# A diffusion layer on one core: the pairs' weight operands in a queue of their own, x's second half modulated on ScalarE, output weights requested one by one

## Chip, core and metric

The kernel runs on one core of one Trainium2 chip. The core has five engines that run their own instruction streams and meet at semaphores: TensorE (PE, matmuls and transposes; its weight loads are shown as PEld), VectorE (DVE), ScalarE (ACT), GpSimd (POOL) and SyncE (SP), which here issues nearly all transfers (DMA). The metric is the device time of one execution in microseconds (us); of several executions the median is taken. A profile of one further execution shows when each instruction ran, for how long, and what ended its engine's idle time before it.

## The reference

One layer over a context of 256 tokens and 2048 latent tokens of width 1024, all in fp32. Cut to what matters:

```python
ada = silu(c) @ w_ada + b_ada                       # six blocks: sh1 sc1 g1 sh2 sc2 g2
h = rmsnorm(x, norm_mix) * (1 + sc1) + sh1          # x: (1, 2048, 1024)
p = h @ w_in                                        # 1024 -> 3584: f, b, v, q, g (512 each), u, v of the gMLP
# head group A: 4 heads of HGRN2, gated linear recurrence, forward and backward, from the context's end states
o_hg = rmsnorm(o_f + flip(o_b), hg_norm) * silu(g)
# head group B: 4 heads of gMLP on chunks of 128 positions
o_mlp = gelu(u) * (W_s @ layernorm(gelu(v)) + b_s)
x = x + g1 * (concat(o_hg, o_mlp) @ w_out)
h2 = rmsnorm(x, norm_ffn) * (1 + sc2) + sh2
a, g = split(h2 @ w_up)                             # 1024 -> 2 x 2816
x = x + g2 * ((a * gelu(conv3x3(g) + conv_b)) @ w_down)
return rmsnorm(x, norm_final)
```

## The kernel before

Matmul operands are split into a high and a low part, each of a short fp32 format (`split`, lines 131 to 134: a cast on ScalarE, then a subtraction on VectorE or GpSimd), and every product is made of three matmuls (hi x hi, hi x lo, lo x hi). The 2048 tokens are worked in two halves of 1024 (`hh` 0 and 1).

The stages, in order of time: norms of the context and of the first half; the input projection, one weight column block of 128 at a time (`load_raw` line 213 loads 512 KB with the transfer of L215, `split_w` casts it into `whi`, `wlo`; matmuls fill PSUM banks `pj`); between these blocks the HGRN2 heads run from a queue of their own (levels L811 to L832, chain of states L860); then the second half, whose gMLP columns come last, as 28 "pair" products, a scheme in the manner of Strassen with seven products for each of four heads, whose weight operands are sums of quarters of `w_in`; then the output projection with `wo`, the FFN's up projection and its convolution, and the down projection.

*Side work.* What isn't on TensorE's main path is written as Python generators, which are queued in a `Pump` (L142). `slot()` (L185) is called between groups of matmuls; each queue then runs its front generator up to its next `yield`. The number given to `yield` is a spacing on the planner's clock of TensorE work, in its microseconds: the queue is not run on before it has passed. There are two queues before the change: `hg_q` for the heads, and `bg_q` for background work. After the first half's second part has begun, `bg_q` is given, one behind the other (L1068 to L1073): `pair_ops` (the pairs' weight operands), eight `ada_block`s (the rest of the adaLN vectors: 64 multiply-adds on VectorE, with weight loads of 512 KB each), `w_out_ops` (output weights times the gate g1, split, stored to `wo_d`), the conv taps, and `w_down_ops` (down weights times g2). Ahead of them in the same queue is `x_second` (L428): it norms, transposes and modulates x's second half, makes sums of its quarters, and stores all to `xo_d`.

*Order.* Generators only set where an instruction stands in its engine's stream; every engine then works through its stream in that order, and waits where an operand or a buffer isn't ready. The SP queue too is one such stream: a transfer that waits for its buffer holds up those behind it.

*Buffers that count.* `raw_tile` (L208): three buffers of 4 KB per partition, shared by the projection's weight loads, the pairs' sums `e`, `ada_block`, `w_out_ops` and `w_down_ops`. The tag `acc`: one buffer, shared by the pairs' `w_hi`, the adaLN accumulator and others. `o_tile` (L760): tag `on`, two buffers. The tag `ot`: two buffers. `wp`: four buffers, in which the pair products' operands are loaded from `sp_d` (`load_pair`, L1185); product n uses buffer n mod 4. `nt`: the gMLP's normalised tile, stored to `oT` at L689 and written anew at L719.

*The end of the second half.* `open_wo` (L1153), called seven products before the last, opens space for `wo` and queues the loads of it (L1170). `wo_early` (L834, L844, L858) opens the first three of the eight `wo` tiles inside the last head. `load_x` refills quarters of x between the products, 1 MB for the high and 1 MB for the low part.

## Time and profile before

| | us |
|---|---|
| median of 3 executions (lowest, highest) | 2518.18 (2517.83, 2522.07) |
| the profiled execution | 2520.09 |
| span of its instructions | 2518.3 |
| TensorE matmuls busy | 2420.5 (96% of the span) |
| VectorE busy | 1846.3 (73%) |
| ScalarE busy | 953.0 (38%) |
| GpSimd busy | 859.2 (34%) |

The profiler's page gives busy times, and the span in 40 equal slices with a digit for the busy tenths of each. "PEclk" is the clock that TensorE was granted, in tenths of full speed (in the tables of stretches as a fraction of 1). A row of a group of instructions reads: line, engine, operation, output <- inputs, shapes, count | busy us in total, mean ns of one | idle time of the engine just before them, with what ended it. A row of waits reads: engine, tile and line that waited <- engine, tile and line that released it: us in total, times, longest. A row of the timeline reads: start us, duration us, engine, line, operation, output <- inputs, count [idle time before <- what ended it]. A row of transfers ends with the number of them, KB of one, and the median us from issue to landing. Lines of helpers stand for all their callers: L133 and L134 are `split`, L65 the matmul, L69 the transpose.

### The profile page before, as it was taken

The page shows a single profiled execution, that of the slowest core. Times are in us where ns is not written, and L with a number is a line of the kernel's source. Part 1 is how long each engine was busy: PE and PEld are TensorE (multiplying, and loading weights), DVE is VectorE, ACT ScalarE, POOL GpSimd, SP SyncE. Part 2 cuts the span into 40 slices and gives each one's busy share as a digit, 9 for nine tenths or more (in the row PEclk, how much of TensorE's full clock was granted, in tenths as well). Part 3 has the DMA queues.
Part 4 walks back from the last instruction along what each step waited for, and adds up shares of the span by engine and source line. Part 5 has one row for each costly group of instructions (what it writes and reads, how often), then busy time and mean ns, then how long its engine had stood idle before and what let it go on. Part 6 is the DMA issues. An engine that isn't in the chain of part 4 may idle for free.

```text
span 2518.3 us, 33045 instructions
## 1 busy us (share of the span) xinstructions
PE 2420.5 (96%) x11811; PEld 2005.0 (80%) x11811; DVE 1846.3 (73%) x2549; ACT 953.0 (38%) x1618; POOL 859.2 (34%) x779
## 2 busy tenths in 40 slices
PE   7998879999999998799999999999999999999998
PEld 4887768888888887588878888888878888888887
DVE  5886766846777775366599787759999994676875
ACT  4553433334344432154443333334333332333243
POOL 1120101111011112100378878878778771000002
PEclk9999989999999999899999999999999999999999
DMA  8486565486354498567852222282222238844745
GB/s 301 129 253 206 195 196 159 131 281 200 106 181 160 140 333 296 200 200 236 293 170 92 85 89 84 91 332 74 91 91 81 91 108 315 324 130 142 230 147 192
DMA packets 351634, 450.50 MB, mean 179 GB/s; under 512 B 34905, under 2 KB 242529, under 8 KB 348397
## 3 DMA queue, kind: packets, MB, share of 16 engines
q1 hardware_dynamic: 348180, 447.62, 53.4%
q8 instruction: 94, 1.54, 0.3%
q10 hardware_dynamic: 3289, 0.76, 0.1%
q14 instruction: 71, 0.58, 0.1%
HBM read 314.01 MB, written 134.29 MB: 178 GB/s over the span
## 4 chain that ended last, share of the span: by engine, by line
PE 41%; DVE 8%; issue 4%; DMA 2%; POOL 2%; ACT 2%; SPq 0%; POOLq 0%; ACTq 0%; DVEq 0%
PE up L65 22%; PE dn L65 18%; DVE dn L1510 3%; DVE edges L1515 1%; DMA yd<-fl 1%; DMA raw<-in_w_up_dram 1%; POOL Al L134 1%; DVE gp L1591 1%; ACT dn L1507 1%; PE up L69 0%; POOL ra L1802 0%; ACT fl L1377 0%; DVE fl L134 0%; POOL rr L1803 0%; DVE cv L1443 0%
## 5 line engine op out<-in xcount | busy, mean ns | idle before, releaser
L1510 DVE SCALAR_TENSOR_TENSOR dn<-gp,taps,dn 128x1024 f32<-128x1024 f32 x352 | 448.6, 1281 | 21.1 <-ACT dn L1507 18.0
L65 PE MATMUL up<-yf,Ah 128*128 128x512 f32 x1232 | 393.8, 389 | 0.0
L65 PE MATMUL dn<-thl,mhl 128*128 128x512 f32 x1680 | 381.5, 389 | 1.2 <-ACT thl L133 1.2
L134 POOL TENSOR_TENSOR Al<-raw,Ah 128x512 fp32r<-128x512 f32 x264 | 342.5, 1306 | 93.2 <-ACT Ah L133 85.2
L65 PEld LDWEIGHTS dn<-thl,mhl 128*128 128x128 f32 x1680 | 315.0, 188 | 67.6 <-ACT thl L133 2.0
L65 PE MATMUL pj<-xh,whi 128*128 128x512 f32 x768 | 312.9, 408 | 17.4 <-ACT whi L133 17.4
L65 PE MATMUL pj<-xh,wlo 128*128 128x512 f32 x768 | 303.0, 395 | 1.8 <-DVE wlo L134 1.7
L65 PE MATMUL pj<-xl,whi 128*128 128x512 f32 x768 | 303.5, 395 | 0.9 <-POOL xl L134 0.8
L65 PE MATMUL up<-xah,Al 128*128 128x512 f32 x704 | 275.7, 392 | 4.9 <-POOL Al L134 4.9
L65 PE MATMUL up<-xah,Ah 128*128 128x512 f32 x704 | 274.9, 391 | 0.6 <-ACT Ah L133 0.6
L65 PEld LDWEIGHTS up<-yf,Ah 128*128 128x128 f32 x1232 | 231.2, 188 | 48.0
L133 ACT CAST Ah<-raw 128x512 fp32r<-128x512 f32 x264 | 160.6, 618 | 276.2 <-PE up L65 213.6
L65 PE MATMUL up<-yf,Al 128*128 128x512 f32 x528 | 205.5, 390 | 0.5 <-POOL Al L134 0.5
L65 PE MATMUL up<-xal,Ah 128*128 128x512 f32 x528 | 205.6, 389 | 0.0
L65 PE MATMUL dn<-wo,o 128*128 128x512 f32 x768 | 184.9, 398 | 0.8 <-DVE nt L727 0.8
L65 PEld LDWEIGHTS pj<-xh,whi 128*128 128x128 f32 x768 | 146.1, 190 | 46.8 <-ACT whi L133 18.0
L65 PEld LDWEIGHTS pj<-xh,wlo 128*128 128x128 f32 x768 | 145.3, 189 | 34.7 <-DVE wlo L134 2.9
L593 POOL TENSOR_TENSOR K<-K,tot 128x512 f32<-128x512 f32 x40 | 52.2, 1305 | 349.9 <-PE sc L65 151.6
L65 PEld LDWEIGHTS pj<-xl,whi 128*128 128x128 f32 x768 | 146.2, 190 | 28.5 <-POOL xl L134 1.7
L65 PEld LDWEIGHTS dn<-wo,o 128*128 128x128 f32 x768 | 144.0, 190 | 30.8 <-DVE nt L727 1.1
L65 PEld LDWEIGHTS up<-xah,Al 128*128 128x128 f32 x704 | 132.1, 188 | 37.5 <-POOL Al L134 10.2
L65 PEld LDWEIGHTS up<-xah,Ah 128*128 128x128 f32 x704 | 132.2, 188 | 28.3 <-ACT Ah L133 1.5
(338 smaller groups left out, 4186.6 us busy)
## 6 DMA issues: line engine op xcount, KB each, us to landing
raw<-in_w_up_dram SPq DMA_DIRECT2D x88, 512.0 KB, 4.7
mr<-m SPq DMA_DIRECT2D x85, 512.0 KB, 5.3
raw<-in_w_in_dram SPq DMA_DIRECT2D x60, 512.0 KB, 4.9
sT<-wd SPq DMA_DIRECT2D x88, 256.0 KB, 4.5
raw<-in_w_ada_dram SPq DMA_DIRECT2D x32, 512.0 KB, 4.0
wp<-sp SPq DMA_DIRECT2D x28, 512.0 KB, 5.0
yf<-yd SPq DMA_DIRECT2D x14, 1024.0 KB
m<-cv SPq DMA_DIRECT2D x22, 544.0 KB, 2.7
```

The lines of the kernel that those rows point to most:

```text
L65: return self.engine.matmul(out, lhsT, rhs, **kw)
L133: keep(S.copy(hi, raw))
L134: (eng or G).tensor_sub(lo, raw, hi.bitcast(F32))
L593: e.tensor_mul(view(K2, row * W + o, src), view(K, o, src), view(tot, t0, [[4, n], [ts, 2], [0, B]]))
L1507: S.activation(cr, gt[:, 0:RH, 0:GW], AF.Identity, bias=cvb[:, f:f + 1], scale=taps[:, f:f + 1])
L1510: V.scalar_tensor_tensor(out=cr, in0=gt[:, t // 3:t // 3 + RH, t % 3:t % 3 + GW], scalar=taps[:, t * NF + f:t * NF + f + 1], in1=cr, op0=A ...
L1515: V.scalar_tensor_tensor(out=e[:, 0, :], in0=gt[:, 1, t % 3:t % 3 + GW], scalar=taps[:, t * NF + f:t * NF + f + 1], in1=e[:, 0, :], op0=AL ...
L1591: V.tensor_add(g_rows(hh, f + c, n2), quad(p, kind), quad(add, kind))
```

## The change

- A third queue, `wp_q`, is run at every `slot()` behind the other two. `pair_ops` goes to it; the adaLN blocks and what follows them in `bg_q` no longer stand behind the pairs. `wp_q` is drained before the second half.
- In `pair_ops` the spacing is 5.0 ahead of the loads, 10.0 (before 6.0) between loads and first use, 2.6 (before 2.0) between the seven steps, and none behind the last. The two sums `e0` and `e1` live in two `o_tile`s instead of one `raw_tile`; `w_hi` in the two buffers of `ot` instead of the one of `acc`.
- In `x_second` the 32 modulations move from VectorE (`tensor_scalar`) to ScalarE (`activation` with scale and bias).
- In the last head of the second half the levels are spaced 3.4 (before 4.2), and 3.0 (before 1.0) stands ahead of its chain.
- `w_down_ops`: 8.0 (before 7.0) between load and use.
- The loads of `wo` in `open_wo` are spaced by 1.2 each, with 5.0 behind them (before: all at once, then 17.0).
- In the pair products `load_pair(n + 3)` is called behind product n and its `load_x`, instead of ahead of product n.

```diff
-    hg_q, bg_q = Pump(), Pump()
+    hg_q, bg_q, wp_q = Pump(), Pump(), Pump()
     def slot():
         hg_q.slot()
         bg_q.slot()
+        wp_q.slot()
...
-                        V.tensor_scalar(out=view(fl, 2 * kk * P, [[1, 256]]), in0=pt[:, kk * 256:kk * 256 + 256],
-                                        scalar1=a1[:, 0, kq:kq + 1], scalar2=s1[:, 0, kq:kq + 1],
-                                        op0=ALU.mult, op1=ALU.add)
+                        S.activation(view(fl, 2 * kk * P, [[1, 256]]), pt[:, kk * 256:kk * 256 + 256], AF.Identity,
+                                     bias=s1[:, 0, kq:kq + 1], scale=a1[:, 0, kq:kq + 1])
...
-                yield 4.2
+                yield 3.4 if (hh, h) == (1, NH - 1) else 4.2
...
-            yield 1.0
+            yield 3.0 if (hh, h) == (1, NH - 1) else 1.0
             chain(fs, False, hf[h], lambda i: tot[:, 1, i:i + 1])
...
                     ld(raw, w_down[2 * j * P:2 * (j + 1) * P, cl].rearrange("(a p) c -> p a c", p=P))
-                    yield 7.0
+                    yield 8.0
...
             for h in range(NH):
+                yield 5.0
                 r0, r1 = (ph.tile([P, D], F32, tag="sgt", name="wr", bufs=2) for i in range(2))
...
-                yield 6.0
+                yield 10.0
                 a11, a12, a21, a22 = r0[:, :512], r0[:, 512:], r1[:, :512], r1[:, 512:]
-                e = raw_tile()
-                e0, e1 = e[:, :512], e[:, 512:]
+                e0, e1 = o_tile(), o_tile()
                 def put(i, t):
-                    hi = pm.tile([P, 512], F32, tag="acc", name="w_hi")
+                    hi = pm.tile([P, 512], F32, tag="ot", name="w_hi", bufs=2)
...
                 V.tensor_add(e0, a21, a22)
                 put(6, a22)
-                yield 2.0
+                yield 2.6
...
                 put(5, a22)
-                yield 2.0
...
-                    bg_q.add(pair_ops())
+                    wp_q.add(pair_ops())
...
+        wp_q.drain()
         seq = []
...
                         ld(wo[k][:, :, sl].bitcast(F32), wo_d[:, k, :, sl])
-                yield 17.0
+                        yield 1.2
+                yield 5.0
...
-            load_pair(n + 2 if n == 0 else n + 3)
             if n == 0:
+                load_pair(2)
                 load_pair(3)
...
                     load_x({0: 3, 1: 4, 2: 6}[m_], op)
+            if n:
+                load_pair(n + 3)
             slot()
```

More of the change, by code (lines that the diff above doesn't have):

```diff
@@ L1011, in pair_ops @@
                 put(6, a22)
-                yield 2.0
+                yield 2.6
                 V.tensor_sub(e1, e0, a11)
                 put(4, e0)
-                yield 2.0
+                yield 2.6
                 V.tensor_sub(a21, a11, a21)
                 put(0, a11)
-                yield 2.0
+                yield 2.6
                 put(3, a21)
-                yield 2.0
+                yield 2.6
                 V.tensor_sub(a22, a12, e1)
                 put(1, e1)
-                yield 2.0
+                yield 2.6
                 put(2, a12)
-                yield 2.0
+                yield 2.6
                 put(5, a22)
-                yield 2.0
         def silu(dst, scale):
```

## The prediction

> **What bounds the kernel now.** I read the page first: busy times and slices.

> ```profile
> span 2518.3 us, 33045 instructions
> PE 2420.5 (96%) x11811; PEld 2005.0 (80%) x11811; DVE 1846.3 (73%) x2549; ACT 953.0 (38%) x1618; POOL 859.2 (34%) x779
> PEclk9999989999999999899999999999999999999999
> ```

> TensorE (PE) sets the time. Nothing of the change takes matmuls away, so it can only win where PE stands idle or runs at a lower clock: the dips are in the first half and near slice 16. So I cut the span at the borders of the work that the change touches and asked for the busy time of each stretch.

> ```profile
> core 0: us, PE busy (x) PEld busy (x) DVE busy (x) ACT busy (x) POOL busy (x), PEclk, DMA share, GB/s
> 116.00:215.00 99.00, 93.41 (x500) 78.19 (x499) 78.63 (x176) 50.24 (x70) 15.72 (x18) 0.98 0.78 233
> 215.00:362.00 147.00, 118.98 (x613) 98.11 (x612) 98.43 (x150) 56.01 (x91) 11.03 (x11) 0.92 0.63 205
> 362.00:500.00 138.00, 138.00 (x774) 118.00 (x773) 105.95 (x141) 51.15 (x80) 19.52 (x18) 1.00 0.48 147
> 500.00:620.00 120.00, 115.83 (x648) 99.25 (x647) 76.89 (x126) 46.79 (x79) 13.20 (x11) 0.99 0.72 244
> 620.00:945.00 325.00, 323.48 (x1898) 282.25 (x1897) 233.75 (x321) 124.38 (x282) 45.68 (x44) 1.00 0.54 184
> 945.00:1072.00 127.00, 101.94 (x512) 84.76 (x512) 58.40 (x159) 22.91 (x61) 25.50 (x32) 0.88 0.68 244
> ```

> Loss is idle time plus busy time done slowly (1 less the clock, times PE busy). Stretch 116 to 215 (x's second half is normalised): 5.6 + 0.02 x 93.4 = 7.5 us. 215 to 362 (pair operands, first adaLN blocks): 28.0 + 0.08 x 119.0 = 37.5. 362 to 500: 0. 500 to 620: 4.2 + 1.2 = 5.4. 620 to 945: 1.5. 945 to 1072 (pairs' products, loads of the output weights): 25.1 + 0.12 x 101.9 = 37.3. What the change can touch is thus about 89 us, 75 of it in two stretches. Next, what ended PE's idle time in these two, the first two rows from 215:362, the others from 945:1072.

> ```profile
> PE pj L65 <- ACT whi L133: 17.4, 3, 10.6
> PE sc L65 <- DVE kd L798: 7.4, 2, 4.3
> PE mi L65 <- DVE nt L719: 15.5, 3, 9.8
> PE pj L65 <- DVE raw L1245: 4.4, 2, 3.0
> ```

> In the first stretch PE mostly waits for the ScalarE cast of a projection weight. Followed back on the timelines of SP, DVE, ACT and PE (each idle time is in brackets):

> ```profile
> 312.39 0.38 SPq L999 DMA_DIRECT2D wr<-in_w_in_dram  x1
> 312.83 0.58 SPq L215 DMA_DIRECT2D raw<-in_w_in_dram  x1
> 316.38 0.69 DVE L1010 TENSOR_TENSOR raw<-wr 128x512 f32<-128x512 f32 x1 [7.85 <-DMA wr<-in_w_in_dram]
> 318.01 1.04 ACT L133 CAST whi<-raw 128x1024 fp32r<-128x1024 f32 x1 [1.00 <-DMA raw<-in_w_in_dram]
> 319.11 0.79 PE L65 MATMUL pj<-xh,whi 128*128 128x512 f32 x1 [10.63 <-ACT whi L133]
> 322.67 0.63 PE L65 MATMUL pj<-xl,whi 128*128 128x512 f32 x1
> 323.10 0.60 PE L65 MATMUL pj<-xh,wlo 128*128 128x512 f32 x1
> 323.77 0.40 PE L65 MATMUL pj<-xl,whi 128*128 128x512 f32 x1
> 324.01 0.39 PE L65 MATMUL pj<-xh,wlo 128*128 128x512 f32 x1
> ```

> The cast is ready 6 us after its weight load was issued; the load was issued late, because on the one SP queue it stands behind the second load of a pair's raw weights. Meanwhile DVE itself stood 7.85 us for that pair load, with all its other work behind it. After the gap matmuls start 0.43 us apart until about 323.5, then 0.24: some 4.4 us at about half rate, 2 us lost beside the gap.

> **The parts and their costs.** The profiled run took 2520.09 us, 1.8 us around its span and 1.9 above the median 2518.18. I sum against 2520.1 and take 1.9 off at the end.

> ```profile
> L454 DVE TENSOR_SCALAR xf<-mi,a,s 128x256 f32<-128x256 f32 x32 | 16.5, 539 | 4.5 <-DMA xo_d<-xf 3.4 <-PE mi L69 1.1
> L1377 ACT ACTIVATE fl<-up,s,a 128x256 f32<-128x256 f32 x56 | 28.4, 558 | 36.4 <-PE up L69 29.2 <-DMA yd<-fl 7.2
> L941 DVE SCALAR_TENSOR_TENSOR acc<-raw,cs,acc 128x512 f32<-128x512 f32 x64 | 48.5, 758 | 4.8 <-DMA acc<-in_b_ada_dram 2.9 <-DMA raw<-in_w_ada_dram 0.6 <-issue 0.5
> L973 DVE TENSOR_TENSOR raw<-raw 128x512 f32<-128x512 f32 x16 | 11.4, 710 | 31.9 <-DMA raw<-g_d 29.0 <-issue 2.9
> raw<-in_w_in_dram SPq DMA_DIRECT2D x60, 512.0 KB, 4.9
> ```

> *x's second half.* 32 x 0.539 = 17.2 us leave DVE; ScalarE gets 32 x 0.558 = 17.9 (L1377 is the same shape, from PSUM with scale and bias). ScalarE is busy 50.2 of the stretch's 99 us, so 68 of 99 fits. DVE comes down from 78.6 to about 62. PE loses 7.5 us here; if DVE's load causes all, 7.5 is won; if instead two of the 16 groups of activations come to stand behind a cast (1.04, above) on ScalarE, 2 is lost. How much of PE's idle time here is due to DVE's load the row does not say, so I take less than half of the gain: 3 won.

> *Pair queue, spacing, buffers.* By the order of instructions in the two built programs, a projection weight load stood only 7, 14, 1 and 1 matmuls ahead of its first use at the four tight places; after, the shortest lead is 26. At 0.23 us a matmul that is 6.0 us against 4.9 to land plus 1.04 to cast: the whi waits (17.4) go, and their slow clock. The adds e0,e1 get tiles of their own, so the pairs no longer hold one of the three raw tiles that the weight loads need; w_hi has two buffers.

> The price: adaLN blocks no longer stand behind the pairs. By the same order, 25 of their 64 DVE instructions and some splits move into the stretch that took 226 to 411 us before, 9 into the stretch ahead of it.

> ```profile
> 226.00:411.00 185.00, 161.31 (x854) 134.24 (x854) 134.27 (x198) 69.62 (x111) 19.94 (x19) 0.94 0.57 184
> 260.00:280.00 20.00, 18.49 (x105) 15.40 (x105) 19.88 (x27) 8.37 (x16) 5.78 (x4) 1.00 0.45 159
> 480.00:500.00 20.00, 20.00 (x114) 16.52 (x113) 18.19 (x25) 7.92 (x11) 3.19 (x3) 1.00 0.35 106
> ```

> PE's own work there is about 145 us: of 185, 23.7 idle and 0.06 x 161.3 = 9.7 slow leave 151.6, and matched against the built order's spacing 144.5; I use 145. DVE's work rises from 134 by 25 x 0.758 = 19 and some 3 of splits to 156. So DVE, not PE, becomes the limit of this stretch. How near to full can it run? The two 20-us rows show 99% with PE losing 1.5 us, and 91% with PE losing nothing. At 95% the stretch takes 164 us, so 21 are won; at 99% 158 (27); at 86% 181 (4). I take 95%, and 2 more from the weight stall at the rim (215 to 226): 23, between 5 and 30. Behind it the load falls (34 adaLN instructions are gone from the time after 411), but w_out's products, whose 29.0 us of waits for g_d PE did not feel, move into it: 0, give or take 5. w_down's spacing of 8.0 is hidden in the flat stretch to 945: 0; uncovered it would be 22 x 1.0.

> *The end.* The rows of 945 to 1072:

> ```profile
> 1005.95 6.78 SPq L1170 DMA_DIRECT2D wo<-wo_d  x9
> 1013.44 0.64 SPq L689 DMA_DIRECT2D oT<-nt  x1
> 1023.21 1.37 DVE L719 TENSOR_SCALAR nt<-mi,mv,rs 128x128 f32<-128x128 f32 x4 [8.52 <-DMA oT<-nt]
> 1023.67 2.08 PE L65 MATMUL mi<-wsT,nt 128*128 128x128 f32 x8 [9.78 <-DVE nt L719]
> 959.12 0.80 PE L65 MATMUL pj<-xh,wp 128*128 128x512 f32 x1 [2.98 <-DVE raw L1245]
> wp<-sp SPq DMA_DIRECT2D x24, 512.0 KB, 5.3
> wo<-wo_d SPq DMA_DIRECT2D x10, 512.0 KB, 10.3
> ```

> Ten wo loads (5 MB) go out in one burst; the store oT<-nt is behind them, its buffer comes free late, DVE waits 8.52 for it and PE 9.78. Requested with 1.2 us between, only two wo loads stand ahead of that store in the new order: 9.8 and about 2 of slow clock can go. The last head's shorter level yields bring its chain of states forward by some 30 matmuls, ahead of the pair sums: 3.0 and 2 of clock. Together up to 17. Against it: the pair operand loads are asked for one product later, behind 2 MB of x. Product 14's load then stands right ahead of its use, and those of 25 to 27 1 to 13 matmuls ahead, for 5.3 us of landing. In fact a load may go when its buffer (product n-1's) is free, so a small lead in the order is not yet a wait; I take 8 off: 9 won, between -7 and 17.

> [...]

> Sum: 3 + 23 + 0 + 9 = 35; 2520.1 - 35 = 2485; less 1.9, **2483**.

> **Rivals.**
> *DVE as the bound makes it slower.* It decides if DVE keeps its idle time while its work grows. DVE idled 185 - 134 = 51 us in 226 to 411; kept whole, the stretch takes 156 + 51 = 207, 22 more, and with only 3 + 9 won elsewhere the time is 2518.2 + 10 = 2528. For: these rows, now with w_out's g_d waits among them.

> ```profile
> DVE raw L1010 <- DMA wr<-in_w_in_dram: 15.9, 3, 7.8
> DVE wr L134 <- ACT w_hi L133: 11.7, 6, 3.5
> ```

> Against: the first is met by 10.0 between load and use instead of 6.0, the second by two buffers. It turns slower beyond 51 - 22 + 12 = 41 us kept.

> *Late pair operands at the end.* SP takes its queue in order, and x's loads wait for the last product that reads the old quarter. Product 14 then waits for 3 MB of x and output weights, 12.9 us at the 244 GB/s of the stretch's row, less the 5.6 that two products of 12 matmuls cover: 7.3. Products 25 to 27 wait for 5.3 less leads of 5, 6 and 13 matmuls: 4.1, 3.9 and 2.3. With 2 of slow clock behind each of the three waits near 4 us or above, 9 turns into 17 - 17.6 - 6 = -7: time 2499.

> *The stalls only move.* The weight loads still share SP with 56 stores that wait for casts; half the whi waits stay, and 23 becomes 11: 2495.

> *It does not do what it says*: the waits are others' and PE merely waits elsewhere, 2518. Against: the chain above is followed instruction by instruction.

> [...]

> **How the numbers follow.** Forecast 60%, own range 2468 to 2496 (the parts' bounds, not all at one end). Late operands 14%, moved stalls 13%, DVE slower 9%, no effect 4%. The range takes in the second and third with their own spread and leaves out the last two: 2463 to 2508. About 0.2%, 5 us, can be told from no change: faster is forecast, late and moved cases, 0.87; the same 0.04; slower 0.09.

> **What would show it.** Right: in 215 to 362 no whi wait over 3 us, clock 0.97 or more, DVE above 90%; PE's waits there name DVE (sc on kd or Q). Near 1010 no 9.78 wait, DVE not on oT<-nt. PE work unchanged. Wrong: pj on DMA wp<-sp in the products (late operands), whi waits beyond 5 us (moved), DVE idle above 40 us with PE waiting (slower).

## The result, and the profile after

The changed kernel took 2488.46 us (median of 4, 2486.64 to 2490.66) against 2520.12 (median of 4) for the kernel before: ratio 0.9873, 95% interval 0.9856 to 0.989, 31.7 us faster. Forecast were 35 us and a time of 2483 (2463 to 2508). A second set of runs gave 0.9864 (0.9844 to 0.9883); its single runs lay up to 8 us apart (2486.99 to 2495.09), and each interval is some 8 us wide, so an edit worth 3 or 4 us can't be told from none here.

The page of the changed kernel, its first lines:

```profile
span 2487.7 us, 33045 instructions
PE 2416.7 (97%) x11811; PEld 2002.9 (81%) x11811; DVE 1827.7 (73%) x2517; ACT 968.2 (39%) x1650; POOL 855.9 (34%) x779
```

The matmuls are the same (x11811) and keep PE busy for nearly the same time (2416.7 us, 2420.5 before); what went is TensorE's idle time and slow time. The table of stretches (length, then busy time of each engine with its instructions, granted clock, share of the transfer engines, GB/s), cut near the same work as before:

```profile
116.00:210.00 94.00, 88.93 (x485) 75.41 (x484) 69.50 (x149) 60.79 (x92) 14.18 (x19) 0.98 0.85 257
210.00:362.00 152.00, 144.72 (x791) 120.07 (x790) 132.11 (x203) 67.68 (x113) 16.82 (x17) 1.00 0.83 266
229.00:386.00 157.00, 149.09 (x838) 124.49 (x837) 144.84 (x220) 67.90 (x109) 21.12 (x20) 1.00 0.75 243
912.00:1045.00 133.00, 114.37 (x557) 95.02 (x557) 59.84 (x163) 24.43 (x64) 25.80 (x34) 0.90 0.72 256
```

The third row holds the matmuls that ran from 226 to 411 us before: 157 us instead of 185, at full clock, with VectorE busy 92% of it (144.84 of 157) instead of 73%. The weight loads are early now. What PE waited for in 210 to 380 us:

```profile
PE sc L65 <- DVE K L593: 1.8, 3, 1.2
...
PE sc L65 <- DVE kd L798: 1.1, 1, 1.1
...
PE pj L65 <- ACT whi L133: 0.2, 1, 0.2
```

The whi waits fell from 17.4 us to 0.2; what is left is mostly short waits for VectorE. From SP's queue, a weight load and behind it a pair load, and below them the cast of that weight on ScalarE's timeline:

```profile
281.56 0.38 SPq L216 DMA_DIRECT2D raw<-in_w_in_dram  x1
287.17 0.38 SPq L1000 DMA_DIRECT2D wr<-in_w_in_dram  x1
```
```profile
285.83 1.05 ACT L133 CAST whi<-raw 128x1024 fp32r<-128x1024 f32 x1 [3.00 <-DMA raw<-in_w_in_dram]
```

The weight load now goes ahead of the pair's loads and not behind them. In the last stretch (912 to 1045 us), PE's waits, and below them its timeline:

```profile
PE mi L65 <- DVE nt L719: 7.9, 3, 4.0
PE pj L65 <- issue: 5.5, 1, 5.5
```
```profile
937.39 0.77 PE L65 MATMUL pj<-xh,wp 128*128 128x512 f32 x1 [5.53 <-issue]
...
1010.01 2.08 PE L65 MATMUL mi<-wsT,nt 128*128 128x128 f32 x8 [4.05 <-DVE nt L719]
1013.02 30.34 PE L65 MATMUL dn<-wo,o 128*128 128x512 f32 x123 [0.93 <-DVE nt L727]
```

The waits of 9.78 and 2.98 us are gone, but a new one of 5.53 us stands ahead of product 14, whose operand load sits behind x's quarters on SP:

```profile
922.11 0.39 SPq L1196 DMA_DIRECT2D xh<-xo_d  x1
922.55 0.50 SPq L1196 DMA_DIRECT2D xl<-xo_d  x1
923.10 3.95 SPq L1190 DMA_DIRECT2D wp<-sp  x1
927.09 1.28 SPq L1224 DMA_DIRECT2D raw<-u  x1
```

The profile names no releaser for this wait ("issue"). But in the trace the operand load of 923.10 reports its landing in sixteen parts from 934.79 to 937.30 us, and the product's first matmul starts at 937.39: it waited for its operand.

To say where the time came from in every kernel, I cut all traces at the same matmuls (those numbered 500, 1020, 1680, 2570, 4090 and 4531 in the built program; the borders lie near 116, 233, 411, 614, 947 and 1076 us before) and subtracted from each part's time what its matmuls need without a gap at full clock, by the planner's spacing. What remains is the loss in us. One profile each; two profiles of the changed kernel differ by about 2 us in a part.

| kernel | to 500 | 1020: x's second half | 1680: pairs, adaLN | 2570 | 4090 | 4531: products | end | sum |
|---|---|---|---|---|---|---|---|---|
| before | 24.1 | 14.1 | 36.3 | 7.8 | 6.1 | 35.0 | 17.6 | 141.0 |
| changed | 25.9 | 9.5 | 15.2 | 6.8 | 4.2 | 29.9 | 19.8 | 111.3 |
| changed, again | 27.0 | 8.8 | 15.3 | 8.1 | 4.3 | 27.9 | 17.7 | 109.1 |

Of the 30 us, 26 come from the two parts with the first weight loads, the pairs and the adaLN blocks, and 5 to 7 from the products.

### The profile page after: what moved, and what is told of

It reads as the page before. It is cut to its first block, busy times and chain, and to the rows that moved or that the text cites. A ratio compares the mean times of both kernels' runs of the same rounds, so it can differ in the third digit from the quotient of the medians.

```text
span 2487.7 us, 33045 instructions
## 1 busy us (share of the span) xinstructions
PE 2416.7 (97%) x11811; PEld 2002.9 (81%) x11811; DVE 1827.7 (73%) x2517; ACT 968.2 (39%) x1650; POOL 855.9 (34%) x779
## 5 line engine op out<-in xcount | busy, mean ns | idle before, releaser
L65 PE MATMUL up<-yf,Ah 128*128 128x512 f32 x1232 | 393.8, 389 | 0.0
L65 PE MATMUL dn<-thl,mhl 128*128 128x512 f32 x1680 | 381.6, 389 | 1.2 <-ACT thl L133 1.2
L134 POOL TENSOR_TENSOR Al<-raw,Ah 128x512 fp32r<-128x512 f32 x264 | 342.8, 1307 | 93.5 <-ACT Ah L133 84.9
L65 PEld LDWEIGHTS dn<-thl,mhl 128*128 128x128 f32 x1680 | 315.0, 188 | 67.7 <-ACT thl L133 2.0
L65 PE MATMUL pj<-xh,whi 128*128 128x512 f32 x768 | 309.9, 404 | 0.2 <-ACT whi L133 0.2
L65 PE MATMUL pj<-xh,wlo 128*128 128x512 f32 x768 | 301.5, 393 | 3.9 <-DVE wlo L134 3.9
L65 PE MATMUL pj<-xl,whi 128*128 128x512 f32 x768 | 302.7, 394 | 0.9 <-POOL xl L134 0.9
L65 PE MATMUL up<-xah,Al 128*128 128x512 f32 x704 | 276.1, 392 | 3.8 <-POOL Al L134 3.7
L65 PE MATMUL up<-xah,Ah 128*128 128x512 f32 x704 | 275.3, 391 | 0.6 <-ACT Ah L133 0.6
L65 PEld LDWEIGHTS up<-yf,Ah 128*128 128x128 f32 x1232 | 231.5, 188 | 48.1
L133 ACT CAST Ah<-raw 128x512 fp32r<-128x512 f32 x264 | 160.7, 618 | 278.2 <-PE up L65 218.8
L65 PE MATMUL up<-yf,Al 128*128 128x512 f32 x528 | 205.4, 389 | 0.5 <-POOL Al L134 0.5
L65 PE MATMUL up<-xal,Ah 128*128 128x512 f32 x528 | 205.7, 390 | 0.0
L65 PE MATMUL dn<-wo,o 128*128 128x512 f32 x768 | 184.6, 397 | 0.9 <-DVE nt L727 0.9
L65 PEld LDWEIGHTS pj<-xh,wlo 128*128 128x128 f32 x768 | 144.4, 188 | 34.8 <-DVE wlo L134 5.2
L65 PEld LDWEIGHTS dn<-wo,o 128*128 128x128 f32 x768 | 143.7, 190 | 30.8 <-issue 1.2
L65 PEld LDWEIGHTS pj<-xh,whi 128*128 128x128 f32 x768 | 144.7, 189 | 29.5 <-issue 2.6
L65 PEld LDWEIGHTS pj<-xl,whi 128*128 128x128 f32 x768 | 144.9, 189 | 28.7 <-POOL xl L134 1.7
L65 PEld LDWEIGHTS up<-xah,Al 128*128 128x128 f32 x704 | 132.4, 188 | 36.5 <-POOL Al L134 8.8
L65 PEld LDWEIGHTS up<-xah,Ah 128*128 128x128 f32 x704 | 132.6, 188 | 28.0 <-ACT Ah L133 1.0
## 6 DMA issues: line engine op xcount, KB each, us to landing
raw<-in_w_up_dram SPq DMA_DIRECT2D x88, 512.0 KB
mr<-m SPq DMA_DIRECT2D x85, 512.0 KB
raw<-in_w_in_dram SPq DMA_DIRECT2D x60, 512.0 KB
raw<-in_w_ada_dram SPq DMA_DIRECT2D x32, 512.0 KB
wp<-sp SPq DMA_DIRECT2D x28, 512.0 KB
```

The costliest lines, as they stand in the source:

```text
L65: return self.engine.matmul(out, lhsT, rhs, **kw)
L133: keep(S.copy(hi, raw))
L134: (eng or G).tensor_sub(lo, raw, hi.bitcast(F32))
```

## The experiments

Theories. (1) The gain is the lead of the projection's weight loads, which the pairs' loads and tiles took away; the rest of the change adds little. (2) VectorE becomes the limit of the pairs' stretch. (3) The end gains little, since pair operands come late. Rivals stand with each run. All ratios are against the kernel before on the same chip.

**Pairs' part alone.** The kernel before with `wp_q`, the new spacing and the new tiles, nothing else.

> The kernel before with the pairs' part of the change alone (own queue, longer spacing, e0/e1 in two o_tiles, w_hi in two buffers). Weight loads held up by the pairs are the cause of most of the gain: 26 to 30 us under the kernel before, 2490 to 2494, no whi wait over 2 us between 210 and 380 us. Rival, VectorE relieved by x's modulation is what lets the pairs' stretch run: under 15 us of gain, PE waiting for VectorE there. Rival, the end carries a third of it or more: gain under 22.

Measured: 2494.68 us, ratio 0.9886 (0.9873 to 0.99), 28.7 us faster. Loss by part, in the order of the table: 24.6, 11.2, 15.5, 10.2, 4.6, 35.4, 15.0. The longest whi wait between 210 and 380 us is 1.0 us. The pairs' part alone makes nine tenths of the gain; the products' loss is that of before (35.4 against 35.0). So the rest of the change adds little, as theory 1 says, and the rival of a large end falls. Whether it is the queue, the spacing or the tiles that does it, this run can't say.

**x's second half on VectorE again.**

```diff
-                        S.activation(view(fl, ...), pt[...], AF.Identity, bias=s1[...], scale=a1[...])
+                        V.tensor_scalar(out=view(fl, ...), in0=pt[...], scalar1=a1[...], scalar2=s1[...], ...)
```

> The changed kernel with x's second half modulated on VectorE again. If that move is worth nothing (the traces show 9.2 us lost from 116 us to the end of x's second half after, 9.7 before): within 2 us of 2488. If it cleared VectorE for the adaLN work that now starts there: 3 to 8 us slower, PE waiting for xf on VectorE and the pairs' stretch longer.

Measured: ratio 0.9873 (0.9856 to 0.989), the same as the changed kernel. Its loss to 1020 is 8.7 us against 9.5 and 8.8, and to 1680 14.3 against 15.2 and 15.3. The move was worth nothing that these runs can tell. The waits of PE between 100 and 225 us, the first row of the changed kernel, the second of this one, show an exchange:

```profile
PE mi L65 <- ACT xf L455: 2.0, 1, 2.0
```
```profile
PE mi L69 <- DVE xk L240: 4.5, 3, 3.4
```

**Pair loads ahead of their product again.**

```diff
+            load_pair(n + 2 if n == 0 else n + 3)
             if n == 0:
-                load_pair(2)
                 load_pair(3)
...
-            if n:
-                load_pair(n + 3)
```

> The changed kernel with load_pair(n + 3) ahead of product n again, as before. If the 5.5 us idle and some 3.5 us of slow clock at product 14 come from pair operands asked for behind x's quarters: both go, 6 to 9 us faster than the changed kernel, near 2480. Rival, x's quarters are then late instead, or the output weights' early loads (1 MB each) fill the transfers anyway: a gap of 3 us or more stays near 930 to 940 us, and the time stays within 2 us of 2488.

Measured: 2486.51 us, ratio 0.9845 (0.9832 to 0.9859); the changed kernel's two intervals overlap it. PE and VectorE on their timelines:

```profile
941.99 0.50 PE L65 MATMUL pj<-xh,wp 128*128 128x512 f32 x1 [4.13 <-DVE raw L1246]
```
```profile
941.24 0.69 DVE L1246 TENSOR_TENSOR raw<-pj,raw 128x512 f32<-128x512 f32 x1 [1.96 <-DMA raw<-u]
```

The 5.53-us wait went, so it was the operand's, and a 4.13-us wait came one product later: now the reload of `u`, next on SP behind the same loads, is late, and the pair sum with it. Ahead of product 26 another reload of `u` costs 3.88 us, against 1.93 in the changed kernel. The transfer engines were full at that moment, and the order seems to decide only which transfer is late; a row of the changed kernel's table of stretches shows it (share 1.04, at 416 GB/s):

```profile
930.00:940.00 10.00, 4.47 (x22) 3.77 (x21) 1.95 (x4) 1.96 (x10) 1.20 (x2) 0.79 1.04 416
```

The loss among the products is 28.9, against 29.9 and 27.9.

**Output weights at once.**

```diff
                         ld(wo[k][:, :, sl].bitcast(F32), wo_d[:, k, :, sl])
-                        yield 1.2
-                yield 5.0
+                yield 17.0
```

> The changed kernel with the ten wo loads requested at once and 17.0 behind them, as before. If the burst ahead of the store oT<-nt made the 9.8 us wait: it is back, VectorE's nt at L719 waits for DMA oT<-nt, 8 to 12 us slower, about 2498. Rival, that wait came from the place of the last head relative to the products and not from the burst: within 3 us of 2488.

Measured: ratio 0.987 (0.9856 to 0.9883), no different from the changed kernel. And yet the wait came back, as the first of the two expectations said; PE, then VectorE's waits:

```profile
993.73 1.65 PE L65 MATMUL mi<-wsT,nt 128*128 128x128 f32 x6 [10.77 <-DVE nt L719]
...
1016.95 13.24 PE L65 MATMUL dn<-wo,o 128*128 128x512 f32 x51 [0.84 <-DVE nt L727]
```
```profile
DVE nt L719 <- DMA oT<-nt: 9.5, 1, 9.5
```

The mechanism was right, its price was not: the output projection starts at 1016.95 instead of 1013.02 us, only 3.9 later, mainly since two pauses of the changed kernel (0.38 and 1.93 us, shown in the last section) are gone. The loss among the products is 34.5 instead of 27.9 to 29.9, and behind them 15.3 instead of 17.7 to 19.8. That last part lay between 15.0 and 19.9 in kernels with either spacing, so whether the delay is really made up there is not shown.

**The changed kernel again.**

> The changed kernel itself, as the measure for the runs beside it: 0.9856 to 0.989 of the kernel before, as first measured.

Measured: 2488.66 us, ratio 0.9864 (0.9844 to 0.9883).

**The queue alone.** The changed kernel with the old `pair_ops`, in `wp_q`.

```diff
-                yield 5.0
...
-                yield 10.0
+                yield 6.0
...
-                e0, e1 = o_tile(), o_tile()
+                e = raw_tile()
+                e0, e1 = e[:, :512], e[:, 512:]
...
-                    hi = pm.tile([P, 512], F32, tag="ot", name="w_hi", bufs=2)
+                    hi = pm.tile([P, 512], F32, tag="acc", name="w_hi")
...
-                yield 2.6
+                yield 2.0
```

> The changed kernel with the old pair_ops (6.0, 2.0, e0 and e1 in one raw tile, w_hi in the one acc buffer), still in the queue of its own. In the built order the projection's weight loads then stand 1 to 13 matmuls ahead of their use at six places. If the lead of these loads is the cause: their waits on whi are back, 15 us or more between 210 and 380 us, and most of the gain is gone: 2508 to 2525. Rival, the queue itself brings the gain, by letting the adaLN blocks go on beside the pairs: within 6 us of the changed kernel.

Measured: 2558.03 us, ratio 1.0133 (1.0114 to 1.0151): 34 us *slower* than before, worse than I expected. The waits of PE in 210 to 400 us:

```profile
PE pj L65 <- ACT whi L133: 23.8, 3, 9.6
PE mi L65 <- DVE acc L941: 21.4, 2, 14.2
```

Now two things interleave that share three raw tiles and one `acc` buffer, and each waits for the other's turn. GpSimd, which clears `acc` for the next adaLN block, gets the buffer only when the store of a pair's `w_hi` out of it has landed, and the 14.2-us wait of PE for this block's `acc` ends 12 us later:

```profile
256.33 0.53 POOL L935 MEMSET acc<- 128x512 f32 x1 [56.34 <-DMA sp<-w_hi]
```

The loss to 1680 is 83.4 us.

**Tiles or spacing.** Two more, each the changed kernel with one half of the old `pair_ops`: the old spacing, and the old tiles.

> The changed kernel with the old spacing of the pairs (6.0 and 2.0, no 5.0 ahead of the loads, 2.0 behind the last step), but its queue and its tiles (e0/e1 in o_tiles, w_hi in two buffers). Three weight loads stand 1 to 3 us of matmul work ahead of their use in the built order, against 5.9 at the least in the changed kernel. If the held raw tile was the main cause: within 8 us of the changed kernel. If the tight places count, each up to 6 us of wait and 2 of slow clock: 12 to 22 us slower, 2500 to 2510, whi waits of 8 us or more.

> The changed kernel with the pairs' old tiles (e in one raw tile, w_hi in the one acc buffer), but its queue and its spacing. Seven weight loads stand 0.2 to 2 us ahead of their use in the built order. If the shared tiles are the main cause: most of the gain is gone, 2515 to 2560, with waits on whi and on acc of 25 us or more. Rival, the spacing is what matters: within 10 us of the changed kernel.

Measured: queue and tiles 2503.08 us, 0.9923 (0.9911 to 0.9935), 21 us under before and some 14 over the changed kernel; queue and spacing 2537.77 us, 1.0058 (1.0046 to 1.007), 14 us over before. Loss to 1680: 29.7 and 54.0, against 15.2 with both and 83.4 with neither; in this part, tiles are worth 54 us without the new spacing and 39 with it, the spacing 29 without the tiles and 14 with them. PE's waits in 210 to 420 us, first the one with tiles, then the one with spacing:

```profile
PE mi L65 <- DVE acc L941: 5.9, 2, 4.6
PE pj L65 <- ACT whi L133: 3.9, 2, 2.2
```
```profile
PE pj L65 <- ACT whi L133: 25.7, 4, 11.6
```

For the kernel with tiles the time came out as expected, the reason only in part: whi waits of 8 us or more were expected and 3.9 came, less than the waits for the adaLN accumulator.

**No queue.** `pair_ops`, with new spacing and tiles, in `bg_q` ahead of the adaLN blocks.

```diff
-                    wp_q.add(pair_ops())
+                    bg_q.add(pair_ops())
...
-        wp_q.drain()
```

> The changed kernel with pair_ops in the background queue again, ahead of the adaLN blocks, with the new spacing and tiles. The weight loads' leads are 35 us and more in the built order. If the leads are the cause: no whi wait over 1 us, within 4 us of the changed kernel or faster, since VectorE's work is less dense there. Rival, the queue is needed: 10 us or more slower.

Measured: 2499.18 us, ratio 0.9902 (0.9886 to 0.9918), 24.4 us under before, some 10 over the changed kernel: the rival's number, but not for its reason. Loss by part: 26.1, 8.3, 3.6, 12.1, 9.0, 44.9, 15.4. The pairs' stretch is nearly without loss (3.6 against 15.2): VectorE is less dense there.

```profile
229.00:386.00 157.00, 154.47 (x887) 133.18 (x887) 123.11 (x190) 71.80 (x117) 20.08 (x17) 1.00 0.58 193
```

The price comes later, in what was pushed back. PE's waits in 900 to 1070 us, and below them SP's queue:

```profile
PE pj L65 <- DMA wp<-sp: 18.2, 4, 8.0
```
```profile
923.93 5.03 SPq L1189 DMA_DIRECT2D wp<-sp  x1
929.00 0.44 SPq L987 DMA_DIRECT2D raw<-in_w_down_dram  x1
```

The down weights' loads (L987) and stores now stand in SP's queue among the pair products' operand loads, and PE waits 18.2 us for these.

**No queue, down weights sooner.** As before, with `w_down` spaced 5.0 and 1.0 (not 8.0 and 2.5), so that it ends ahead of the products, and the pair loads ahead of their product.

> The kernel without the own queue (new spacing and tiles kept), with w_down spaced 5.0 and 1.0 instead of 8.0 and 2.5, and the pair loads asked for ahead of their product. The queue's worth is then that w_down's 22 MB of transfers are done before the pair products: last store at matmul group 3914 here, 3732 in the changed kernel, 4347 without the queue. If so, the 18.2 us of waits for wp<-sp are gone, the dense stretch keeps its small loss, and it is the fastest yet: 2472 to 2482. Rival, quicker w_down work crowds the stretch from 640 to 900 us: no faster than the changed kernel.

Measured: 2487.52 us, ratio 0.9853 (0.984 to 0.9866): not told apart from the changed kernel, so the expected 2472 to 2482 failed. Loss by part: 27.1, 8.5, 2.7, 12.5, 13.8, 28.6, 19.9. The late operands are cured (no wait for wp is left, the loss is 28.6), though two edits share this, the spacing of `w_down` and the order of the pair loads. The pairs' stretch is the best of all (2.7), and 15 us more than in the changed kernel are lost from 1680 to 4090, into which adaLN, output and down weights are now pressed.

**adaLN multiply-adds doubled.**

```diff
                     V.scalar_tensor_tensor(out=acc, in0=wt[:, i, :], scalar=cs2[:, k + i, 0:1], in1=acc,
                                            op0=ALU.mult, op1=ALU.add)
+                    V.scalar_tensor_tensor(out=wt[:, i, :], in0=wt[:, i, :], scalar=cs2[:, k + i, 0:1], in1=wt[:, i, :],
+                                           op0=ALU.mult, op1=ALU.add)
```

> The changed kernel with every adaLN multiply-add done a second time into its own weight tile, which nothing reads: 64 more VectorE instructions of about 0.76 us, some 19 of the 49 us in the dense stretch of 229 to 386 us, where VectorE was busy 92% of the time. If VectorE is the limit of that stretch: 15 to 25 us slower in it, PE waiting for VectorE; by room left (12 us idle) at least 7. Rival, VectorE is not the limit and its lag is absorbed by work that PE does not wait for: under 5 us slower.

Measured: 2513.53 us, ratio 0.9954 (0.9939 to 0.997), 25 us over the changed kernel. Loss to 1680: 33.9 instead of 15.2, to 2570: 17.4 instead of 6.8 to 8.1. The stretch, and below it PE's waits there:

```profile
229.00:403.00 174.00, 152.64 (x803) 126.05 (x802) 166.16 (x256) 65.41 (x107) 21.65 (x20) 0.94 0.67 216
```
```profile
PE pj L65 <- ACT whi L133: 9.7, 4, 4.9
PE mi L65 <- DVE acc L941: 5.2, 3, 3.2
```

VectorE is busy 95% (166.16 of 174). PE's longest wait here names ScalarE's cast, but it begins with VectorE. SP's queue stood from 287.4 to 291.38 us for a pair's store, whose tile VectorE finished at 291.36, and the weight load behind it went out only then:

```profile
290.68 0.68 DVE L134 TENSOR_TENSOR on<-on,w_hi 128x512 fp32r<-128x512 f32 x1
291.38 0.32 SPq L1011 DMA_DIRECT2D sp<-on  x1
292.46 0.41 SPq L216 DMA_DIRECT2D raw<-in_w_in_dram  x1
297.96 0.79 PE L65 MATMUL pj<-xh,whi 128*128 128x512 f32 x1 [4.89 <-ACT whi L133]
```

About half of the added 64 x 0.76 = 49 us is paid. So theory 2 holds in this form: the changed kernel stands near VectorE's limit there, with some room left.

**Last head's yields as before** (4.2 and 1.0).

> The changed kernel with the last head's yields as before (4.2 and 1.0). If the shorter ones bring its chain of states forward, ahead of the pair sums: the 3 us wait of pj on VectorE's pair sum is back, and 3 to 6 us are lost. Rival, the product-14 wait for its operand covers the same time anyway: within 2 us of the changed kernel.

Measured: 2483.77 us, ratio 0.9849 (0.9832 to 0.9866), not slower. The loss among the products is 26.4, the least of all. Two of PE's waits on a pair sum, ahead of products 15 and 26, and VectorE just before the second:

```profile
930.01 0.50 PE L65 MATMUL pj<-xh,wp 128*128 128x512 f32 x1 [1.01 <-DVE raw L1246]
989.05 0.79 PE L65 MATMUL pj<-xh,wp 128*128 128x512 f32 x1 [5.98 <-DVE raw L1246]
```
```profile
988.30 0.69 DVE L1246 TENSOR_TENSOR raw<-pj,raw 128x512 f32<-128x512 f32 x1 [4.44 <-DMA raw<-u]
```

The expected wait did come back, ahead of product 15 as in the kernel before, with the sum behind the chain of states on VectorE; but it is 1.01 us long and not 2.98. The long one is another: there VectorE waits for the reload of `u`. The 5.53-us operand wait isn't there (the longest for an operand is 0.73). In the built order the second and third early loads of `wo`, which follow the last head, stand some 60 and 30 matmuls later than in the changed kernel, so the operands may go ahead of them; that this is the reason was not shown. The time is the rival's: the shorter yields bought nothing that can be told.

## Why the prediction was right

*Pair queue, spacing, tiles: 23 us forecast, 26 measured* (the losses to 1020 and to 1680 fell from 50.4 to 24.7). The reason was the named one: whi waits from 17.4 to 0.2 us, clock from 0.92 to 1.00. That VectorE becomes the limit was nearly right, as the doubled multiply-adds show; of the signs named, its share above 90% holds from 229 to 386 us (92%), not from 215 to 362 (128.68 of 147 us, 88%). Mis-sized was its busy time: 156 us forecast, 144.84 measured. 25 more multiply-adds did move in (28 before, 53 after). But the durations of all its instructions in the stretch rose by 15.6 us (146.1 to 161.7) and not by 22, since no more splits came with them; and its busy time rose by only 10.6, since records of instructions that follow each other at once overlap, which adding durations leaves out (161.7 us added, 144.84 busy). The stretch took 157 us, not 164, at 92% and not 95%. What the text didn't separate, the runs did: the tiles are the larger half, and the queue, which lets adaLN run beside the pairs, is a loss of 34 us without both, a loss of 14 with the spacing alone and a gain of 21 with the tiles alone. The queue's own worth seems to lie elsewhere than I looked: with it the down weights end ahead of the products, and without it PE waited 18.2 us for operands there.

*x's second half: 3 forecast, 0 measured.* Failed step: that VectorE's load causes PE's losses there. 17 us of modulations came off it (its busy time fell only from 78.63 to 69.50 and not to 62, since 8 of the adaLN multiply-adds that the prediction moves ahead run there), PE waited 2.0 us for ScalarE instead, and the 4.6 us by which this part lost less came also with the modulation on VectorE (8.7). They fit the end of the part, where PE waited 4.3 us for kd before and no longer does.

*w_out and w_down: 0 forecast.* The parts to 2570 and 4090 changed by +0.3 to -1.9.

*The end: 9 forecast, 5 to 7 measured.* The 9.78 and 2.98 waits went as said. The 8 us that I took off for late operands came as one wait of 5.53 at product 14, with its slow clock (0.50 from 935.73 to 942.56 us); those of products 25 to 27 were 0.38 us at most for an operand. Failed was the reading of two waits as prices. Put back, the 9.8 us delay the output projection by 3.9, mainly since two other pauses go; and the 3.0 us and 2 of slow clock, which the last head's yields were to save, are a wait of 1.01 us with the old yields.

That the sum of 35 came near 31.7 is in part luck: 23 came out as 26, 3 as 0 and 9 as 5 to 7, and these errors partly cancel.

*The slower rival* was a real one: not in this kernel, but in the queue without tiles and spacing (2558), where the same matmuls took from 233 to 457 us and VectorE idled 74 of these 224 us, against 51 of 185 before. In the sums for the end, the forecast set 2 us of slow clock behind each wait of 3.0 us and more, and none behind shorter ones. In the changed kernel, gaps of 1.72 and 0.38 us, and one of 1.93, were each time followed by a clock of 0.50 (below).

What stays open: whether single edits at the end are worth 0 or 4 us each; the intervals of the changed kernel, of pair loads ahead and of the old yields overlap. These three and the last kernel without the queue were not combined.

## To carry to other kernels

Before background work gets a queue of its own, look which buffers it shares with what it will now run beside: here the same queue, the rest of the change alike, was 34 us slower with shared tiles and 32 faster with its own tiles and wider spacing. For each load that the bounding engine needs, read its lead off the built order and set it against the load's landing and cast time (4.9 and 1.04 us in the kernel before); in the kernels with leads of 0.2 to 3 us the stalls came back, and 5.9 us was enough. It was enough only while buffers came free in time: with VectorE's work doubled, the same order had whi waits of 9.7 us. A wait taken off the end of a stage full of transfers was worth less than its length here, since the next transfer in line was then the late one (pair loads ahead: 5.53 us went and 4.13 came one product later; the transfer engines' share there was 1.04 in the changed kernel).

## What the runs showed of the hardware

Behind gaps of 1.72 and 0.38 us, and behind one of 1.93, TensorE's clock stood at 0.50. In the changed kernel's timeline of PE:

```profile
985.25 1.45 PE L65 MATMUL mi<-wsT,nt 128*128 128x128 f32 x8 [1.72 <-DVE nt L719]
987.08 0.79 PE L65 MATMUL pj<-xh,wp 128*128 128x512 f32 x1 [0.38 <-DMA wp<-sp]
...
990.98 0.39 PE L65 MATMUL pj<-xl,wp 128*128 128x512 f32 x1
991.21 0.39 PE L65 MATMUL pj<-xh,wp 128*128 128x512 f32 x1
993.53 0.62 PE L65 MATMUL pj<-xh,wp 128*128 128x512 f32 x1 [1.93 <-DVE raw L1246]
993.95 0.63 PE L65 MATMUL pj<-xl,wp 128*128 128x512 f32 x1
```

Before the 1.93-us gap the starts are 0.23 us apart, behind it 0.42, until 997.2. In the dense stretch from 229 to 386 us, with 7.9 us of idle time in waits of at most 1.4 us, the clock stayed at 1.00.

```profile
983.52:986.93 3.41, 1.46 (x9) 1.19 (x8) 2.31 (x6) 0.00 (x0) 2.38 (x3) 1.00 1.04 412
986.93:990.34 3.41, 3.26 (x8) 2.59 (x9) 0.56 (x1) 0.00 (x0) 0.00 (x0) 0.50 1.04 411
990.34:993.76 3.42, 1.49 (x7) 0.93 (x6) 0.87 (x2) 0.00 (x0) 0.00 (x0) 1.00 1.05 408
993.76:997.17 3.41, 3.41 (x9) 2.63 (x9) 0.51 (x1) 0.63 (x1) 1.28 (x1) 0.50 1.04 411
```

And one of the kernel before, around a gap of 2.79 us (987.50 to 990.30):

```profile
985.73:989.14 3.41, 1.77 (x10) 1.14 (x8) 2.59 (x12) 0.60 (x1) 1.45 (x3) 1.00 1.01 395
989.14:992.55 3.41, 2.25 (x13) 1.94 (x14) 3.41 (x15) 0.00 (x0) 0.15 (x1) 1.00 1.03 408
```

From 60 us to the last matmul, these two traces have 15 steps at full clock in which PE idled for 1.93 us or more in all, 9 before and 6 after the change; each was followed by a step at half rate. In the other steps at full clock it idled for 1.71 us at most, and none was followed by one. The 2.79-us gap fell into two steps, 1.64 us of it into the first and 1.16 into the second, and the clock stayed at 1.00; the 1.93-us gap fell into one. So in these two traces the clock followed the idle time summed over a step and not the length of one gap.
